# Modulation vectors of the second block: narrow products on TensorE, or dot products on VectorE in other stages

## The chip, the cores and the metric

The kernel runs on one core of one Trainium2 chip. The metric is the time of one execution on the device in microseconds (us), the median of several runs. Engines carry the profile's names: PE is TensorE's matmul, PEld its weight load, DVE is VectorE, ACT is ScalarE, POOL is GpSimd, SP is SyncE, which here only issues DMAs. L83 is line 83 of the kernel; the change shifts line numbers by a few, so that the same statement has another number afterwards.

## The reference, cut to what matters

A first block (a state-space mixer "s5" and a gated recurrence of 8 heads "hgrn2", merged, then a gated feed-forward stage) turns x and 16 meta tokens into x1. The second block modulates x1 and a context by vectors that come from two condition vectors of 1024 numbers each: `c` for the tokens, `c_ctx` for the context.

```python
def _adaln(cond, w_mod, b_mod):
    m = jax.nn.silu(cond) @ w_mod + b_mod        # w_mod: 1024 x 3072
    return jnp.split(m, 3, axis=-1)              # shift, scale, gate
...
        if i % 2 == 0:                           # layer "ab"
            sh, sc, gt = _adaln(c, ab_w_mod[j], ab_b_mod[j])
            h = x * (1.0 + sc[:, None]) + sh[:, None]
            ...
                csh, csc, cgt = _adaln(c_ctx, ab_w_mod[j], ab_b_mod[j])
                hc = ctx * (1.0 + csc) + csh
        else:                                    # layer "cd"
            csh, csc, cgt = _adaln(c_ctx, cd_w_mod[j], cd_b_mod[j])
            hc = ctx * (1.0 + csc) + csh
            sh, sc, gt = _adaln(c, cd_w_mod[j], cd_b_mod[j])
```

So four vectors of 3072 numbers are wanted: `c` and `c_ctx` through the ab weights, `c` and `c_ctx` through the cd weights. Of the last the gate is never used. None depends on x: they can be computed at any time before their use.

## The kernel before, in words

Features lie on the 128 partitions, tokens on the columns. Every float32 product is made of three float32r products: weights and inputs are split into a rounded part and a rest. `split_w` loads a raw 128x1024 tile into the pool `wraw` (two buffers; the DMA is issued by SP at L74), ACT copies its rounded part (L75), and DVE subtracts that from the raw tile (L76). `panel` then multiplies one such tile with all tokens (`mm3`, L83): 72 matmuls for the three token chunks of the first block, 24 for the 256 tokens of the context.

The stages of the program, in order:

- `s5`: eight passes. Each projects an input (one panel of L83), stores it to DRAM and reads it back in another layout, and DVE builds a table `ctab` (five operations, the last at L368) that PE transposes (L438). A scan over chunks on DVE and eight output passes end the stage.
- `hgrn`, the heads: eight heads, each with two panels of its own, a DVE chain (two scans over 1040 columns, L598 and L599, reciprocals, some twenty products, states), and about a hundred small matmuls; at its end DVE scales the output `o`, and SP stores it to `YBd` (L729). The second scan of the next head writes the tile `B`, which is the buffer of `o`: it waits until that store has landed. Other panels (`z_panel`: queries, values and gates wanted later) fill PE's time in the heads and after them; their number is fixed, so a panel that is done in a head is not to be done later.
- `ctx_path`: the context through layer ab and half of cd. Its own panels are small, and `fill` puts a `z_panel` between them.
- `merge`, `ffn` (ten groups of `up` and `down`; `up` is two panels and a convolution of three DVE operations per panel, `down` adds products into the residual on DVE at L951), then the second block on the tokens.

Around the change: `mods` is a generator that `hgrn` advances six times per head. For each of 48 tiles (2 layers x 3 parts x 8 input blocks) it loads 128 inputs x 1024 features into the pool `wm` (two buffers, L1015) and multiplies them with both conditions: the conditions, padded to 32 columns, are the stationary operand, and the weights stream past in four matmuls of 256 columns (L1017; in the trace eight records per tile). After eight tiles DVE copies the sums out, PE transposes them (L1024), and DVE adds the bias and forms 1 + scale and gate / ALPHA (L1027, L1029).

Each engine runs its instructions in one fixed order, and so does each queue of DMA issues. That order comes from the scheduler of the tile framework: it places every instruction by the data and buffers that it needs and by the order of the code, so an edit in one place can move instructions of others.

Of the kernel before, what the change touches and what calls it, by code (L numbers as in the profile page):

```python
# [19 lines left out]
NJ = 1026  # L20
# [17 lines left out]
class Build:  # L38
# [20 lines left out]
    # ---- weights: raw -> exact split into two float32r parts  # L59
# [8 lines left out]
    # the sources side by side into the two parts of t  # L68
# [9 lines left out]
    # X: function (part, k, lo, hi) -> AP ; W: tile [128, 2, nk*128]  # L78
# [18 lines left out]
    # rsqrt(ps * scale + eps), one Newton step on top of the table's value  # L97
# [30 lines left out]
    # exp(x) in place on a small tile, x clamped to [-87, 88]  # L128
# [26 lines left out]
    # sin(th + shift) with the range brought to [-pi, pi]; shift 0 or pi/2  # L155
    def exact_sin(self, pool, out, th, shape, shift):
# [25 lines left out]
    # ================= block 1 =================  # L182
# [20 lines left out]
    def block1(self, upto):  # L203
# [32 lines left out]
        # panel 1 (queries), 2 (values) of a head; 0: gates  # L236
# [33 lines left out]
    # panels chunk by chunk, where the chunks of X come one after the other  # L270
# [7 lines left out]
    def s5_params(self, pool, w1):  # L278
# [37 lines left out]
        # powers a^0..a^8, ascending (pa) and descending (pd)  # L316
# [18 lines left out]
        # bb = coef * b  # L335
# [10 lines left out]
        # scan multipliers [Ar|Ar], [-Ai|Ai]  # L346
# [7 lines left out]
    def cmul_tab(self, pool, pw, r0, r1, co, i):  # L354
        """out[128, 2, 4, 8, 16] = pw (over t) * co (over h) for the four pairs of panel i"""
# [15 lines left out]
    def s5(self):  # L371
# [5 lines left out]
        with ExitStack() as es:  # L377
# [17 lines left out]
            # first panels token chunk by token chunk, under the norm of the next chunk  # L395
# [3 lines left out]
            for c, (lo, hi) in enumerate(CH1):  # L399
                pss = [self.ps_mm()[:, 0:hi - lo] for _ in ws]  # L400
                # as the inputs of the first chunk come
# [18 lines left out]
            proj(2)  # L420
            for i in range(8):
                if i < 5:
                    proj(i + 3)
# [7 lines left out]
                # maps  # L431
# [28 lines left out]
                # chunk inputs to the states  # L460
# [7 lines left out]
            # outputs' factors, real and imaginary states on top of each other  # L468
# [6 lines left out]
            # scan over the chunks  # L475
# [9 lines left out]
            # outputs  # L485
            for i in range(8):
# [7 lines left out]
                # re(a^t c) over -im(a^t c)  # L494
# [24 lines left out]
    # ---- hgrn2  # L519
    def hgrn(self):  # L520
        nc, tc, A = self.nc, self.tc, self.A
        v = nc.vector
        with ExitStack() as es:
# [37 lines left out]
            wm = es.enter_context(self.pool("wm", 2, side="right"))  # L561
            mods = self.mods(wm, hp)
            for hd in range(8):
                # projections
# [5 lines left out]
                next(mods, None)  # L570
# [4 lines left out]
                next(mods, None)  # L575
                next(mods, None)
# [7 lines left out]
                next(mods, None)  # L584
                next(mods, None)
                next(mods, None)
# [6 lines left out]
                # decays inside the chunks of 16  # L593
# [16 lines left out]
                # queries and keys against the middle of their chunk of 32; QI: block, key chunk, query  # L610
# [3 lines left out]
                # meta chunk  # L614
# [8 lines left out]
                # chunk totals  # L623
# [9 lines left out]
                # queries decayed from the start of their chunk of 32, then from the middles of earlier chunks  # L633
# [7 lines left out]
                # products over the chunks of 16 before and after in the block of 128  # L641
# [36 lines left out]
                # states before each block  # L678
# [12 lines left out]
                # outputs  # L691
# [19 lines left out]
                # norm over the head's features, gate  # L711
                # (four token ranges side by side in the columns of the array, brought back by selections)
# [20 lines left out]
            for m in mods:  # L733
                pass

    # exact split of an fp32 tile into the two parts of t[:, :, lo:hi]
# [13 lines left out]
    # a product whose result goes on to a norm: the first panels panel by panel, the last nres  # L750
    # panels token chunk by token chunk, so that the norm of a chunk runs under the next chunk.
    # sq: the norm needs the sum of squares (else the plain sum) over all panels' rows r(i, lo, hi);
    # done(c, lo, hi, ps) gets that sum in every partition
# [68 lines left out]
    def merge(self):  # L822
# [5 lines left out]
        with ExitStack() as es:  # L828
# [50 lines left out]
            # h1 = h + (2 m) @ w_out / 2, then its norm  # L879
# [3 lines left out]
            # in place of the product's input, which a finished chunk no longer needs  # L883
# [19 lines left out]
    def ffn(self):  # L903
# [5 lines left out]
        with ExitStack() as es:  # L909
# [58 lines left out]
            for gi, js in enumerate(groups):  # L968
                for j in js[0:2]:
                    up(j)  # L970
                if gi:
                    down(groups[gi - 1], False)
# [21 lines left out]
    def mods(self, pool, cp):  # L994
# [13 lines left out]
        for which in ("ab", "cd"):  # L1008
            m = self.mod[which] = self.const.tile([128, 24, 2], F32, name=f"mod_{which}")
            bm = self.load(self.const, f"{which}_b_mod")  # L1010
            for part in range(3):
                ps = self.ps_sm()[:, 0:256]
                for k in range(8):
# [4 lines left out]
                    if k < 7:  # L1018
                        yield
# [793 lines left out]
```

## Time and profile before

| | |
|---|---|
| time, median of 3 runs | 3249.68 us (3247.68 to 3250.23) |
| span of the profiled execution | 3242.6 us, that is 7.1 us less than the median |
| PE busy | 3165.4 us, 98% of the span |
| DVE, ACT, POOL busy | 1831.4, 1126.1, 92.9 us |
| heads (first to last store of `YBd`) | 477.1 to 783.6 us |

The span runs from the first to the last instruction; the 7.1 us around it are outside the trace. In rows of a stretch the columns are its bounds, its length, then for PE, PEld, DVE, ACT and POOL the busy time (with the number of instructions), then the granted TensorE clock (1.00 is full speed), the busy share of the DMA engines and GB/s. In a timeline a row is the start, the time from the first start to the last end, engine, line and what it writes and reads; rows of the same kind in succession are put together with their count, and brackets give idle time before it and what ended it.

### The profile page before, as it was taken

The page shows a single profiled execution, that of the slowest core. Times are in us where ns is not written, and L with a number is a line of the kernel's source. Part 1 is how long each engine was busy: PE and PEld are TensorE (multiplying, and loading weights), DVE is VectorE, ACT ScalarE, POOL GpSimd, SP SyncE. Part 2 cuts the span into 40 slices and gives each one's busy share as a digit, 9 for nine tenths or more (in the row PEclk, how much of TensorE's full clock was granted, in tenths as well). Part 3 has the DMA queues.
Part 4 walks back from the last instruction along what each step waited for, and adds up shares of the span by engine and source line. Part 5 has one row for each costly group of instructions (what it writes and reads, how often), then busy time and mean ns, then how long its engine had stood idle before and what let it go on. Part 6 is the DMA issues. An engine that isn't in the chain of part 4 may idle for free.

```text
span 3242.6 us, 47786 instructions
## 1 busy us (share of the span) xinstructions
PE 3165.4 (98%) x19986; PEld 2840.8 (88%) x19986; DVE 1831.4 (56%) x3508; ACT 1126.1 (35%) x1846; POOL 92.9 (3%) x99
## 2 busy tenths in 40 slices
PE   8999899999999999999999999999999999999998
PEld 6999887879999999999999999989997889555476
DVE  7549468775454334465554555455336464777744
ACT  5341733233344312232222222252224353544532
POOL 0000000000210000000000000000000000121100
PEclk9999999999999999999999999999999999999999
DMA  4342454343552234111111111111111223000211
GB/s 153 90 161 91 148 182 142 118 153 103 158 155 81 91 118 130 33 59 46 40 46 53 47 52 40 53 35 54 46 40 66 92 88 130 29 7 7 79 49 52
DMA packets 106384, 269.01 MB, mean 83 GB/s; under 512 B 14798, under 2 KB 43694, under 8 KB 105974
## 3 DMA queue, kind: packets, MB, share of 16 engines
q1 hardware_dynamic: 99656, 245.35, 23.3%
q10 hardware_dynamic: 4464, 16.34, 1.3%
q0 software_dynamic: 2048, 4.26, 0.7%
q8 instruction: 157, 2.57, 0.3%
q14 instruction: 59, 0.48, 0.0%
HBM read 219.12 MB, written 46.11 MB: 82 GB/s over the span
## 4 chain that ended last, share of the span: by engine, by line
PE 90%; DVE 4%; DMA 2%; ACT 2%; issue 1%; SPq 0%; DVEq 0%; ACTq 0%
PE mm L83 62%; PE mm L949 7%; PE sm L1558 4%; PE mm L1555 4%; PE sm L813 2%; PE mm L1124 2%; PE sm L1531 1%; DMA YBd<-o 1%; PE mm L1516 1%; ACT Tt L502 1%; DVE R L604 1%; PE sm L465 1%; PE sm L1573 0%; PE sm L708 0%; PE sm L1017 0%
## 5 line engine op out<-in xcount | busy, mean ns | idle before, releaser
L83 PE MATMUL mm<-z,whl 128*128 128x256 f32 (+3 forms) x4032 | 682.9, 325 | 1.5 <-ACT z L231 1.0
L83 PE MATMUL mm<-a,whl 128*128 128x384 f32 (+1 forms) x4320 | 682.7, 319 | 1.6 <-ACT u L917 1.6
L83 PEld LDWEIGHTS mm<-a,whl 128*128 128x128 f32 x4320 | 678.5, 188 | 3.7 <-ACT u L917 1.9
L83 PEld LDWEIGHTS mm<-z,whl 128*128 128x128 f32 x4032 | 637.6, 189 | 36.8 <-issue 29.2
L76 DVE TENSOR_TENSOR whl<-wraw,whl 128x1024 fp32r<-128x1024 f32 (+2 forms) x258 | 302.6, 1178 | 221.1 <-ACT whl L75 220.3
L75 ACT CAST whl<-wraw 128x1024 fp32r<-128x1024 f32 (+2 forms) x258 | 260.6, 1014 | 341.8 <-PE mm L949 137.0
L83 PE MATMUL mm<-hx,whl 128*128 128x384 f32 (+1 forms) x2232 | 366.3, 322 | 7.7 <-ACT fx L1378 7.1
L83 PEld LDWEIGHTS mm<-hx,whl 128*128 128x128 f32 x2232 | 352.0, 189 | 16.8 <-ACT fx L1378 7.3
L949 PE MATMUL mm<-g,whl 128*128 128x384 f32 (+1 forms) x1584 | 257.9, 322 | 2.3 <-DVE f L951 1.2
L949 PEld LDWEIGHTS mm<-g,whl 128*128 128x128 f32 x1584 | 248.0, 188 | 13.9 <-issue 8.1
L83 PE MATMUL mm<-b,whl 128*128 128x384 f32 (+1 forms) x1152 | 180.9, 319 | 0.0
L83 PEld LDWEIGHTS mm<-b,whl 128*128 128x128 f32 x1152 | 180.8, 189 | 0.0
L917 ACT COPY u<-mm 128x384 f32<-128x384 f32 x132 | 58.3, 445 | 317.8 <-PE mm L83 317.8
L951 DVE TENSOR_TENSOR f<-f,mm 128x384 f32<-128x384 f32 (+1 forms) x240 | 118.3, 508 | 71.3 <-PE mm L949 70.4
L1556 ACT ACTIVATE P<-mm 128x512 f32<-128x512 f32 x160 | 94.7, 597 | 134.4 <-PE mm L1555 127.9
L83 PEld LDWEIGHTS mm<-y,whl 128*128 128x128 f32 x816 | 120.2, 188 | 13.1 <-issue 9.8
L83 PE MATMUL mm<-y,whl 128*128 128x256 f32 (+1 forms) x816 | 128.1, 312 | 1.4 <-ACT y L741 1.1
L1558 PE MATMUL sm<-P,m 128*64 128x512 f32 x320 | 128.0, 611 | 0.6 <-ACT P L1556 0.5
L1532 DVE TENSOR_REDUCE mx<-sm 128x1 f32<-128x512 f32 (+1 forms) x192 | 105.7, 595 | 39.7 <-PE sm L1531 38.4
L1555 PE MATMUL mm<-m,KB 97*128 97x512 f32 x420 | 121.7, 405 | 0.0
L1555 PEld LDWEIGHTS mm<-m,KB 97*128 97x128 f32 x420 | 75.6, 188 | 47.4 <-issue 33.3
L923 DVE TENSOR_SCALAR av<-u,conv_w,conv_b 128x1024 f32<-128x1024 f32 x22 | 17.9, 812 | 138.7 <-ACT u L917 138.7
(519 smaller groups left out, 3664.0 us busy)
## 6 DMA issues: line engine op xcount, KB each, us to landing
wraw<-w_up SPq DMA_DIRECT2D x44, 512.0 KB, 3.2
wraw<-w_h SPq DMA_DIRECT2D x32, 512.0 KB, 3.4
wraw<-ab_w SPq DMA_DIRECT2D x32, 512.0 KB, 3.4
wm<-ab_w_mod SPq DMA_DIRECT2D x24, 512.0 KB
wm<-cd_w_mod SPq DMA_DIRECT2D x24, 512.0 KB, 4.0
wraw<-w_down SPq DMA_DIRECT2D x22, 512.0 KB, 3.2
ut<-Ud SPq DMA_DIRECT2D x16, 520.0 KB, 4.5
gt<-Gd SPq DMA_DIRECT2D x16, 513.0 KB, 3.2
```

The source lines that it names most:

```text
L75: self.nc.scalar.copy(t[:, 0], raw)
L76: self.nc.vector.tensor_tensor(out=t[:, 1], in0=raw, in1=t[:, 0].bitcast(F32), op=ALU.subtract)
L83: nc.tensor.matmul(ps, W[:, wp, wofs + 128 * k:wofs + 128 * k + 128], X(xp, kofs + k, lo, hi), start=first and k == 0 and i == 0, stop=las ...
L813: nc.tensor.matmul(p4[32 * j:32 * j + 32], self.ones[:, 0:32], x, start=i < 4, stop=i - len(pend) + j + 5 >= m)
L917: return u, (self.split_w(A["w_up"][p], [1024]), lambda c, lo, hi, ps: nc.scalar.copy(u[:, lo:hi], ps))
L949: nc.tensor.matmul(ps, ws[j][:, wp, 128 * o:128 * o + 128], G[j][:, xp, lo:hi], start=n_ == 0 and i == 0, stop=n_ == len(js) - 1 and i == 2)
L951: v.tensor_tensor(out=h1[o][:, 2 + lo:2 + hi], in0=h1[o][:, 2 + lo:2 + hi], in1=ps, op=ALU.add)
L1124: nc.tensor.matmul(ps, X(xp, k, 128 * t, 128 * t + 128), wv[k // 4][:, wp, 256 * (k % 4):256 * (k % 4) + 256], start=k == 0 and i == 0, st ...
L1532: v.tensor_reduce(out=mx[:, qt, j:j + 1], in_=ps, axis=mybir.AxisListType.X, op=ALU.max)
L1555: nc.tensor.matmul(ps, K[0:97, kp, 128 * t:128 * t + 128], Q[0:97, qp, 512 * c:512 * c + 512], start=i == 0, stop=i == 2)
L1556: nc.scalar.activation(Pt[:, c], ps, AF.Exp, scale=scale)
L1558: nc.tensor.matmul(po[64 * c:64 * c + 64, :], vv(t)[:, 64 * h:64 * h + 64], Pt[:, c], start=t == 0, stop=t == KT - 1)
```

## The change

The vectors are formed on DVE: the weights now come transposed, 128 features on the partitions and the 1024 inputs on the columns, and one `tensor_tensor_reduce` multiplies such a tile with the condition (the same row in all partitions), sums over the columns, adds the bias, and writes one column of the result. A tile serves one condition only. It appears in the program as two DVE instructions, one of 128x1024 and one of 128x1. `mods` is advanced in three stages: in `s5` three tiles per pass (ab for `c_ctx`, 24 tiles, in the buffers `km`), in `ctx_path` three per `fill` (cd for `c_ctx` without the gate, 16 tiles, in the `wraw` buffers of the z panels), in `ffn` three per `up` (all six parts for `c`, 48 tiles, in `wraw`). That makes 88 tiles of 512 KB in place of 48. Each stage prepares its condition row with `cond_rows`. The rest of the difference is comments that went.

```diff
@@ s5 @@
             proj(2)
+            self.mod_start()
+            cr = self.cond_rows(w1.tile([128, 1024], F32, tag="ys", name="cr1", bufs=1), w1.tile([128, 1024], F32, tag="k2", name="crt", bufs=1), 1)
+            mods = self.mods([("ab", 0), ("ab", 1), ("ab", 2)], 1, cr, lambda: w1.tile([128, 1024], F32, tag="km", name=self.nm("wm")))
             for i in range(8):
+                for _ in range(3):
+                    next(mods)
@@ hgrn @@
-            wm = es.enter_context(self.pool("wm", 2, side="right"))
-            mods = self.mods(wm, hp)
...
-                next(mods, None)
-                next(mods, None)
...
-            for m in mods:
-                pass
@@ ffn @@
+            cr = self.cond_rows(wx.tile([128, 1024], F32, tag="whl", name="cr3"), tp.tile([128, 1024], F32, tag="acc", name="crt", bufs=3), 0)
+            mods = self.mods([(w, p) for w in ("ab", "cd") for p in range(3)], 0, cr,
+                             lambda: self.wraw.tile([128, NJ], F32, tag="wraw", name=self.nm("wm"))[:, 0:1024])
...
                     up(j)
+                    for _ in range(3):
+                        next(mods, None)
@@ mods @@
-                    nc.sync.dma_start(w, A[f"{which}_w_mod"][8 * part + k])
-                    for j in range(4):
-                        nc.tensor.matmul(ps[32 * j:32 * j + 32], cs[:, k], w[:, 256 * j:256 * j + 256], start=k == 0, stop=k == 7)
...
+    def cond_rows(self, t, tmp, col):
+        nc.sync.dma_start(t, self.A["cond"][col].partition_broadcast(128))
+        nc.scalar.activation(tmp, t, AF.Tanh, scale=0.5)
+        v.scalar_tensor_tensor(out=t, in0=tmp, scalar=1.0, in1=t, op0=ALU.add, op1=ALU.mult)
+        v.tensor_scalar(out=t, in0=t, scalar1=0.5, scalar2=None, op0=ALU.mult)
+        return t
+    def mods(self, todo, col, c, new):
+        for which, part in todo:
+            m = self.mod[which]
+            for f in range(8 * part, 8 * part + 8):
+                w = new()
+                nc.sync.dma_start(w, A[f"{which}_w_mod"][f])
+                v.tensor_tensor_reduce(out=w, in0=w, in1=c, scale=1.0, scalar=self.modb[which][:, f:f + 1],
+                                       op0=ALU.mult, op1=ALU.add, accum_out=m[:, f, col:col + 1])
+                if f % 8 == 7 and part:
+                    o = m[:, 8 * part:8 * part + 8, col]
+                    v.tensor_scalar(out=o, in0=o, scalar1=(1.0, 1.0 / ALPHA)[part - 1], scalar2=None, op0=(ALU.add, ALU.mult)[part - 1])
+                yield
@@ ctx_path @@
+            cr = self.cond_rows(cp.tile([128, 1024], F32, name="cr2", tag="csq"), wg.tile([128, NJ], F32, tag="wraw", name="crt")[:, 0:1024], 1)
+            mods = self.mods([("cd", 0), ("cd", 1)], 1, cr, lambda: wg.tile([128, NJ], F32, tag="wraw", name=self.nm("wm"))[:, 0:1024])
+            fill0 = fill
+            def fill():
+                fill0()
+                for _ in range(3):
+                    next(mods, None)
             self.ab_mixer(tp, yp, X, T, CH, half_out, fill)
+            list(mods)
+            fill = fill0
@@ inputs @@
-        D[f"{w}_w_mod"] = np.ascontiguousarray(f(f"{w}_w_mod_2")[0].reshape(8, 128, 3, 1024).transpose(2, 0, 1, 3)).reshape(24, 128, 1024)
+        D[f"{w}_w_mod"] = np.ascontiguousarray(f(f"{w}_w_mod_2")[0].T).reshape(24, 128, 1024)
```

Where it moves instructions. PE at the end of the last head: `ry` is the last head's 1 / deviation, `z_83` to `z_90` the eight tiles of the normed input, each `whl` the weights of a panel. Before:

```order
L727 MATMUL sm_7606<-ry_7594,idr 128x258
L727 MATMUL sm_7610<-ry_7594,idr 128x258 x2
L83 MATMUL mm_7817<-z_85,whl_7785 128x384
L83 MATMUL mm_7817<-z_86,whl_7785 128x384 x3
L83 MATMUL mm_7817<-z_87,whl_7785 128x384 x3
L83 MATMUL mm_7817<-z_88,whl_7785 128x384 x3
```

Now:

```order
L724 MATMUL sm_7340<-ry_7328,idr 128x258
L724 MATMUL sm_7344<-ry_7328,idr 128x258 x2
L83 MATMUL mm_7662<-z_87,whl_7604 128x386
L83 MATMUL mm_7662<-z_88,whl_7604 128x386 x3
L83 MATMUL mm_7662<-z_89,whl_7604 128x386 x3
L83 MATMUL mm_7662<-z_90,whl_7604 128x386 x3
```

Between these last matmuls of the heads and the first panel on the context (`hc`) stand 184 panel matmuls before, and 82 now (the ten shown in part and one panel of 72); the other 102 stand inside the heads now.

DVE in `s5`, at the first table `ctab` (`ctmp` is its scratch tile; `wm`, `cr_818` and `mod_ab` are a weight tile, the condition row and the result). Before:

```order
L365 TENSOR_TENSOR ctab_991<-ctab_991,ctmp_992 128x512
L363 TENSOR_TENSOR ctab_1153<-pd,bb 128x512
L367 TENSOR_TENSOR ctmp_992<-pd,bb 128x512
L366 TENSOR_TENSOR ctab_1153<-pd,bb 128x512
L368 TENSOR_TENSOR ctab_991<-ctab_991,ctmp_992 128x512
```

Now:

```order
L365 TENSOR_TENSOR ctab_1012<-ctab_1012,ctmp_1013 128x512
L366 TENSOR_TENSOR ctab_1012<-pd,bb 128x512
L367 TENSOR_TENSOR ctmp_1013<-pd,bb 128x512
L1022 ISA wm_1083,mod_ab<-wm_1083,cr_818,ab_b_mod_813 128x1024
L1022 ISA mod_ab 128x1
L368 TENSOR_TENSOR ctab_1012<-ctab_1012,ctmp_1013 128x512
```

The two operations on the second table went behind L368, and the fifth weight tile came ahead of it; four more such pairs and the two operations on the condition row stand further up.

DVE in `ffn`, in a down phase (`f` are tiles of the residual, `mm` sums of PE in PSUM). Before:

```order
L951 TENSOR_TENSOR f_12709<-f_12709,mm_15871 128x384
L951 TENSOR_TENSOR f_12803<-f_12803,mm_15879 128x384
L951 TENSOR_TENSOR f_12803<-f_12803,mm_15887 128x256
L76 TENSOR_TENSOR whl_16002<-wraw_16003,whl_16002 128x1024
L951 TENSOR_TENSOR f_12803<-f_12803,mm_15895 128x384
```

Now:

```order
L946 TENSOR_TENSOR f_12791<-f_12791,mm_14648 128x384
L1022 ISA wm_14901,mod_ab<-wm_14901,cr_13169,ab_b_mod_813 128x1024
L1022 ISA mod_ab 128x1
L946 TENSOR_TENSOR f_12791<-f_12791,mm_14656 128x256
L946 TENSOR_TENSOR f_12791<-f_12791,mm_14664 128x384
```

Of the six weight tiles of a group two stand between the 24 evictions of its down phase, the other four in the up phases.

## Rows read from the trace of the kernel before

**Rows 1.** The page: busy time by engine; the chain that ended last.

```profile
PE 3165.4 (98%) x19986; PEld 2840.8 (88%) x19986; DVE 1831.4 (56%) x3508; ACT 1126.1 (35%) x1846; POOL 92.9 (3%) x99
...
PE 90%; DVE 4%; DMA 2%; ACT 2%; issue 1%; SPq 0%; DVEq 0%; ACTq 0%
```

**Rows 2.** Groups by line, 423 to 783 us: busy us, mean ns, idle before.

```profile
L1017 PE MATMUL sm<-wm,conds 128*32 128x256 f32 x384 | 36.5, 389 | 7.1 <-DMA wm<-ab_w_mod 5.0 <-DMA wm<-cd_w_mod 2.1
```

**Rows 3.** Line L1017: what ended PE's idle time (us, times).

```profile
  DMA wm<-ab_w_mod: 10.4, 9
  DMA wm<-cd_w_mod: 6.8, 13
```

**Rows 4.** Timeline of PE, 440 to 455 us: start, duration, line, count.

```profile
441.97 0.64 PE L1017 MATMUL sm<-wm,conds 128*32 128x256 f32 x8
442.54 1.31 PE L83 MATMUL mm<-z,whl 128*128 128x384 f32 x6
```

**Rows 5.** Stretches from one store to the next: length, engines' busy, clock, DMA.

```profile
477.10:522.90 45.80, 42.26 (x368) 34.85 (x360) 33.87 (x68) 14.87 (x21) 0.00 (x0) 1.00 0.50 150
...
567.10:613.70 46.60, 42.45 (x336) 39.01 (x335) 34.61 (x69) 15.52 (x23) 0.00 (x0) 0.93 0.24 69
...
746.70:783.60 36.90, 35.88 (x297) 33.50 (x296) 22.62 (x40) 12.36 (x19) 0.00 (x0) 1.00 0.25 87
```

**Rows 6.** Waits of DVE, 423 to 783 us: total, times, longest.

```profile
DVE B L599 <- DMA YBd<-o: 34.3, 7, 6.2
DVE SC L704 <- PE sm L703: 11.4, 8, 2.9
```

**Rows 7.** Timeline of SP's issues, 743 to 753 us.

```profile
746.65 0.33 SPq L729 DMA_DIRECT2D YBd<-o  x1
748.27 0.33 SPq L74 DMA_DIRECT2D wraw<-w_g  x1
```

**Rows 8.** Timeline of DVE, 743 to 753 us.

```profile
746.49 0.17 DVE L1027 TENSOR_TENSOR mod_cd<-sm,cd_b_mod 128x16 f32<-128x16 f32 x1
...
751.16 2.33 DVE L599 TENSOR_TENSOR_SCAN B<-fm,dr 128x1040 f32<-128x1040 f32 x1 [2.95 <-DMA YBd<-o]
```

**Rows 9.** Timeline of PE, 564 to 586 us.

```profile
583.87 1.94 PE L671 MATMUL sm<-ident,B 128*128 128x128 f32 x8 [3.95 <-DVE B L660]
```

**Rows 10.** Timeline of PE, 780 to 815 us.

```profile
782.39 29.92 PE L83 MATMUL mm<-z,whl 128*128 128x384 f32 x184
```

**Rows 11.** Groups of DVE by form, 423 to 783 us.

```profile
L604 DVE RECIPROCAL R<-B 128x512 f32<-128x512 f32 x8 | 26.8, 3352 | 0.2
...
L598 DVE TENSOR_TENSOR_SCAN F<-fm,fr 128x1040 f32<-128x1040 f32 x8 | 18.5, 2317 | 0.0
```

**Rows 12.** Groups of DVE by form, 1400 to 2090 us.

```profile
L924 DVE SCALAR_TENSOR_TENSOR ag<-u,conv_w,ag 128x1024 f32<-128x1024 f32 x22 | 28.3, 1284 | 0.8
```

**Rows 13.** The page, costliest groups: a TENSOR_SCALAR of 1024 columns.

```profile
L923 DVE TENSOR_SCALAR av<-u,conv_w,conv_b 128x1024 f32<-128x1024 f32 x22 | 17.9, 812 | 138.7 <-ACT u L917 138.7
```

**Rows 14.** Timeline of DVE, 85 to 101 us.

```profile
94.07 0.68 DVE L366 TENSOR_TENSOR ctab<-pd,bb 128x512 f32<-128x512 f32 x1
94.67 0.68 DVE L368 TENSOR_TENSOR ctab<-ctab,ctmp 128x512 f32<-128x512 f32 x1
```

**Rows 15.** Timeline of PE, 95 to 101 us.

```profile
100.26 0.93 PE L438 MATMUL sm<-ident,ctab 128*128 128x128 f32 x7
```

**Rows 16.** Stretches of s5, of ctx_path and of one down phase.

```profile
100.00:200.00 100.00, 99.73 (x841) 92.81 (x841) 36.78 (x90) 38.89 (x71) 0.00 (x0) 1.00 0.39 103
900.00:1000.00 100.00, 98.86 (x722) 93.50 (x721) 57.45 (x116) 55.14 (x86) 8.38 (x16) 1.00 0.43 134
1746.20:1769.20 23.00, 23.00 (x147) 22.84 (x146) 17.39 (x29) 2.83 (x4) 0.00 (x0) 1.00 0.08 24
```

**Rows 17.** Timeline of PE, 812 to 850 us.

```profile
817.75 11.54 PE L83 MATMUL mm<-z,whl 128*128 128x256 f32 x72
...
835.09 11.54 PE L83 MATMUL mm<-z,whl 128*128 128x256 f32 x72
```

More of the change, by code (lines that the diff above doesn't have):

```diff
@@ L574, in hgrn @@
                 nc.scalar.activation(k, k, AF.Identity, scale=fbn[:, hd:hd + 1], bias=fb[:, hd:hd + 1])
-                next(mods, None)
-                next(mods, None)
                 for j, t in ((1, q), (2, vv)):
@@ L583, in hgrn @@
                         self.panel(w, self.zx, 8, CH1 if j == 2 else CHT, lambda c, lo, hi, ps: nc.scalar.copy(t[:, lo:hi], ps))
-                next(mods, None)
-                next(mods, None)
-                next(mods, None)
                 w = self.split_w(A["w_h"][4 * hd + 3], [1024])
@@ L991, in x1_chunk, with mod_start @@
             self.split_act(self.hx[k], lo, hi, t)
-    def mods(self, pool, cp):
+    def mod_start(self):
+        self.mod = {}
+        self.modb = {}
+        for which in ("ab", "cd"):
+            self.mod[which] = self.const.tile([128, 24, 2], F32, name=f"mod_{which}")
+            self.modb[which] = self.load(self.const, f"{which}_b_mod")
+    def cond_rows(self, t, tmp, col):
+        nc = self.nc
+        v = nc.vector
+        nc.sync.dma_start(t, self.A["cond"][col].partition_broadcast(128))
[3 more added lines that the diff above has]
+        return t
@@ L997, in mods @@
+    def mods(self, todo, col, c, new):
         nc, A = self.nc, self.A
         v = nc.vector
-        self.mod = {}
-        cd = self.load(self.const, "cond")
-        th = self.const.tile([128, 16], F32, name="condt")
-        nc.scalar.activation(th, cd, AF.Tanh, scale=0.5)
-        v.scalar_tensor_tensor(out=cd, in0=th, scalar=1.0, in1=cd, op0=ALU.add, op1=ALU.mult)
-        v.tensor_scalar(out=cd, in0=cd, scalar1=0.5, scalar2=None, op0=ALU.mult)
-        cs = cp.tile([128, 8, 32], F32, name="conds")
@@ L1006, in mods @@
-        v.memset(cs, 0.0)
-        v.tensor_copy(cs[:, :, 0:2], cd.rearrange("p (k c) -> p k c", c=2))
[L1008 to L1013, printed above, removed]
-                    w = pool.tile([128, 1024], F32, tag="wm", name=self.nm("wm"))
-                    nc.sync.dma_start(w, A[f"{which}_w_mod"][8 * part + k])
-                    for j in range(4):
-                        nc.tensor.matmul(ps[32 * j:32 * j + 32], cs[:, k], w[:, 256 * j:256 * j + 256], start=k == 0, stop=k == 7)
-                    if k < 7:
-                        yield
-                e = pool.tile([128, 1024], F32, tag="wm", name=self.nm("me"))[:, 0:256]
-                v.tensor_copy(e, ps)
-                pt = self.ps_sm()
-                for h in range(2):
-                    nc.tensor.transpose(pt[:, 128 * h:128 * h + 128], e[:, 128 * h:128 * h + 128], self.ident)
-                o = m[:, 8 * part:8 * part + 8].rearrange("p (j h) c -> p h j c", h=2)
-                b = bm[:, 8 * part:8 * part + 8].rearrange("p (j h) -> p h j", h=2).unsqueeze(3).to_broadcast([128, 2, 4, 2])
-                v.tensor_tensor(out=o, in0=pt[:, 0:256].rearrange("p (h j c) -> p h j c", h=2, j=4)[:, :, :, 0:2], in1=b, op=ALU.add)
-                if part:
-                    v.tensor_scalar(out=m[:, 8 * part:8 * part + 8], in0=m[:, 8 * part:8 * part + 8], scalar1=(1.0, 1.0 / ALPHA)[part - 1],
-                                    scalar2=None, op0=(ALU.add, ALU.mult)[part - 1])
@@ L1031, in mods @@
                 yield
-            self.dump("mod_" + which, m)
     def ln_chunk(self, tp, r, ps, n, emit, sqt, tail):
@@ L1223, in ctx_path @@
                 ps = add(k, x[:, k])
-            sqs = cp.tile([128, 4, T], F32, name="csq")
+            sqs = cp.tile([128, 4, T], F32, name="csq", tag="csq")
             self.ln_chunk(tp, lambda k: x[:, k], ps, T, emit, lambda k: sqs[:, k % 4], 0)
@@ L1740, in prep @@
     D["fin_g"] = pk(f("final_norm_g"))
-    D["cond"] = np.ascontiguousarray(np.stack([pk(f("c_2")[0]), pk(f("c_ctx_2"))], 2).reshape(128, 16))
+    D["cond"] = np.ascontiguousarray(np.stack([f("c_2")[0].reshape(1024), f("c_ctx_2").reshape(1024)], 0))
     for w in ("ab", "cd"):
-        D[f"{w}_w_mod"] = np.ascontiguousarray(f(f"{w}_w_mod_2")[0].reshape(8, 128, 3, 1024).transpose(2, 0, 1, 3)).reshape(24, 128, 1024)
+        D[f"{w}_w_mod"] = np.ascontiguousarray(f(f"{w}_w_mod_2")[0].T).reshape(24, 128, 1024)
         D[f"{w}_b_mod"] = pk(f(f"{w}_b_mod_2")[0])
```

## Prediction, made before the changed kernel had run

> **What bounds the kernel now.** I read the page first. PE is busy for 98% of the span, and the chain that ended last runs 90% through PE and 4% through DVE [rows 1]: whatever comes off PE's work or its idle time is a gain, and DVE, busy for 56%, costs something only where PE waits for it. Next came the groups of the heads, where the removed products stand: 384 matmul records of L1017, 36.5 us busy [rows 2]. Busy time of pipelined matmuls overlaps with the neighbours', so I take the price from the timeline: the eight records of a tile start at 441.97, and the next panel matmul starts at 442.54, 0.57 us later [rows 4]. 48 tiles are 27.4 us of PE. Before them PE also idled for 10.4 and 6.8 us, until their weights had landed [rows 3], 17.2 us. Together 44.6 us, which is the most that PE can get back from the removal.
>
> Then I asked whether PE is what a head waits for. From one store of `YBd` to the next a head takes 45.8 or 46.6 us, with PE busy 42.3 and 42.5 and DVE 33.9 and 34.6 [rows 5]; the mean of the six from 477.1 to 746.7 is 44.93. Neither engine is full. DVE's waits name the chain: it stood 34.3 us before its second scan, until the store of the head before had landed [rows 6], and 11.4 us for PE's scores (L704). The head is a chain store, scan, DVE, PE, DVE, store, with panels around it. [...]
>
> **What goes, in the heads.** (1) The store's wait. In six heads the weight loads stand in SP's queue beside the store, and the scan waited (34.3 - 2.95) / 6 = 5.2 us. Around the last store, at 746.65, SP issued no `wm` load, only a panel's weights [rows 7], and the scan waited 2.95 us [rows 8]. I take the last head's wait for all: 6 x 2.3 = 13.6 us (bounds: 0, as loads of panel weights remain in the queue, to 6 x 5.2 = 31). (2) DVE's waits for PE, where weight products stood ahead of a head's own ones: bounds 0 and 11.4; I take 0.6 us a head, 3.4 in six, near the lower end, since the head with hardly any of these products was no faster. (3) The end. Between the last head's matmuls and the context's first panel stand 184 panel matmuls before and 82 now, as the order shows. The 184 took 29.92 us [rows 10], so 102 of them are 16.6 us that are no longer to be done there; PE does them in the heads, 14 or so a head. That PE has the time: 42.4 - 27.4 / 8 + 14 x 0.163 = 41.3 us of work against 44.9 - 2.8 = 42.1 per head. What now hides the context's first DVE operations behind the last head is 82 matmuls, 13.3 us, in place of 184; by bounds that costs 0 to 5, I take 0. The heads give 13.6 + 3.4 + 16.6 = 33.6, below the ceiling of 44.6.
>
> **What comes: one tile on DVE.** No row shows a multiply that sums over its columns. From below: a TENSOR_SCALAR of 1024 columns takes 0.81 us [rows 13]; from above: the RECIPROCAL, 3.35 us for 512 columns, so 6.7 for 1024 [rows 11]. Between them a SCALAR_TENSOR_TENSOR of 1024 columns with two float32 sources takes 1.28 [rows 12] and a scan over 1040, which carries a sum along, 2.32 [rows 11]. The nearest in operands and length is the 1.28; with 0.17 for the second instruction, of one column, as for an operation of 16 columns [rows 8], I take p = 1.45 us per tile, 88 tiles, 128 us of DVE work in all.
>
> [...]
>
> **s5.** DVE finishes the first table at 94.67 + 0.68 = 95.35 [rows 14] and PE, which has panels to do, takes it up at 100.26 [rows 15]: 4.9 us in hand. Ahead of it now stand the condition's two operations (1.28 + 0.81) and five tiles, while two operations of the second table (0.6 apart) went behind: 2.1 + 5p - 1.2 - 4.9 = 5p - 4.0, 3.3 us at p = 1.45; I take 4, as two buffers hold five tiles and the third to fifth wait for a load (bounds 0 and 10). The other passes: DVE is busy 36.8 of 100 us and PE 99.7 [rows 16]; a pass is a panel of 72 and some 60 smaller matmul records, and 841 took 100 us, so it takes 15.7, of which DVE has 9.9 free and gets 3p = 4.4. Cost 0 up to p = 3.3. Behind a weight load that waits for its buffer SP queues the input panel's weights and the eight stores of the pass; PE is behind them only when that wait is longer than a panel.
>
> **ctx_path.** A panel in front of 48 context matmuls, 817.75 to 835.09, is 17.3 us [rows 17], and DVE is busy 57.5 of 100 [rows 16], 10 of these 17.3; three tiles are 4.4 more, 14.4 of 17.3. It fits up to p = 2.5, but evictions stand in the queue behind the tiles, and the z panels' weights share their two buffers with them; 0 to 8 us, I take 2.5.
>
> **ffn.** A down phase of 23.0 us has DVE busy for 17.4 [rows 16], 5.6 free, and two tiles, 2.9 us, now stand between its 24 evictions; the other four stand where DVE waits for a panel. PE has four PSUM buffers, so that one delayed eviction doesn't stop it. Fits up to p = 2.8; 0 to 5 us, I take 0.5.
>
> **The sum.** -33.6 + 4 + 2.5 + 0.5 = -26.6 us, against the profiled execution: 3242.6 - 26.6 = 3216.0 of span; with the 7.1 us that the median has beyond this span 3223.1, so 3223 us. If each term is off by the bounds that I find plausible, this case runs from 3213 to 3233.
>
> **Rivals.** A, the head's chain is DVE's own and loads of panels keep the store as late as before: periods stay 44.9, only the end's 16.6 us remain, less 7 is -9.6: 3240. For it: the head at 567.1, long without weight tiles; against it: its clock was low, and the last store's wait was short. If PE idles more in the heads and all six get the clock of that one, 1.7 us each (46.6 - 44.9), it ends at 3250, no change.
>
> B, the new instruction is long, and DVE becomes the bound. Place: s5, the context and the down phases. Price: 5p - 4 at the first table, 16 tiles of ctx_path beyond 2.5, 16 tiles in down phases beyond 2.8, 19 in s5 beyond 3.3, and 2.5. It equals 33.6 at p = 3.2, from which point the kernel is slower; at p = 4 it is 16 + 24 + 19 + 13 + 2.5 = 75, and 3250 - 34 + 75 = 3291 us. For it only that the operation is unknown, and the RECIPROCAL's 3.35 for half the columns; against it the two-source row at 1.28.
>
> C, PE gets everything back, 44.6, and the additions hide but for 3 us at the first table: 3208. For it PE's 98%; against it DVE's 34 us of work and the store's latency in each head.
>
> D, SP's queue: a weight load that waits for DVE holds back the loads and stores behind it, and PE waits for the panel's weights at each of the 24 tiles of s5 as it did for a weight tile in the heads, 10.4 / 9 = 1.2 us [rows 3]: 28 us, the gain is gone: 3251. Against it: PE's 99.7% there says that its weights come early [rows 16].
>
> **How the numbers follow.** Chances: forecast 0.50, C 0.14, A 0.20, B 0.08, D 0.08. This kernel's measurement can tell 0.2%, 6.5 us, from no change. Faster takes all of the forecast and of C, 0.12 of A and 0.02 of D: 0.78. Same takes 0.05 of A and 0.03 of D: 0.08. Slower is B with 0.03 each of A and D: 0.14. The range for 8 in 10 goes from C's far side, 3204, to the top of A without a low clock, 3246.
>
> **What would show it.** In the trace after: no L1017; stores of `YBd` about 42 us apart and the scan's wait near 3 us (in A 45 and 5); a panel stretch of some 13 us behind the last head in place of 29.9; L1022 at about 1.3 us (in B over 3); PE idle before L438's counterpart, about 4 us; DVE at 83% in ctx_path with PE still at 98%; down phases still 23 us. The prediction is wrong if the tile takes over 2.5 us, or if a head's period is above 44.

## The result: 1% slower, where 0.8% faster was forecast

The changed kernel takes 3280.48 us (median; 3278.04 to 3285.44), the kernel before, run beside it, 3248.68. The ratio is 1.0108 (95% interval 1.0093 to 1.0122), outside the range and on the other side. The profiled execution has a span of 3283.6 us, 41.0 more than before. It is the longest of its four executions, and the one before, to judge by its span, the shortest of its four (3244.17 us), so the stretches below add up to 9 us more than the 31.8 between the medians.

The page of the kernel after, busy time by engine and the chain that ended last, answering to [rows 1]:

```profile
PE 3148.6 (96%) x19590; PEld 2848.1 (87%) x19590; DVE 1938.4 (59%) x3677; ACT 1131.5 (34%) x1849; POOL 93.6 (3%) x99
...
PE 83%; DVE 8%; DMA 5%; ACT 3%; issue 2%; SPq 0%; DVEq 0%; ACTq 0%
```

PE's busy time fell by 17 us, and it is busy for 96% of the span in place of 98%; 8% of the chain runs through DVE and 5% through DMAs, where they had 4 and 2. Work went and waits came. To see where, I take the first or last start of one line in each stage (views of one line) and subtract before from after:

| stretch | before | after | change | forecast |
|---|---|---|---|---|
| start to the first output product of s5 | 362.9 | 406.4 | +43.5 | +4 |
| from there over the heads to the context's first panel | 449.2 | 413.0 | -36.2 | -33.6 |
| ctx_path, first to last panel on the context | 178.0 | 196.9 | +18.9 | +2.5 |
| ffn, first copy of `u` to first eviction of a down phase | 75.4 | 93.0 | +17.6 | +0.5 with the next |
| all the rest | 2177.1 | 2174.3 | -2.8 | 0 |

**The heads did what was forecast.** From 518.4 to 769.4 a head takes 41.8 us on average (42.1 was forecast). First one such stretch, answering to [rows 5], then the waits of DVE for the store, answering to [rows 6], then the panels behind the last head, answering to [rows 10]:

```profile
518.40:559.20 40.80, 37.97 (x312) 35.38 (x311) 34.59 (x67) 15.45 (x23) 0.00 (x0) 1.00 0.23 66
```

```profile
DVE B L596 <- DMA YBd<-o: 23.2, 7, 5.0
```

```profile
806.23 13.28 PE L83 MATMUL mm<-z,whl 128*128 128x386 f32 x82
```

The scan waited 23.2 us for the stores in place of 34.3, and 82 panel matmuls take 13.28 us in place of 184 in 29.92.

**The new instruction costs what was forecast.** The view of its line; duration min/median/max, then what its engine waited for:

```profile
L1022 DVE CUSTOM_DVE_ANT_0 wm<-wm,cr,ab_b_mod x48: 1270/1284/1286, 84.9 to 1628.9; 128x1024 f32<-128x1024 f32 x48
L1022 DVE DVE_READ_ACCUMULATOR2_ANT mod_ab<- x48: 75/84/86, 86.1 to 1630.1; 128x1 f32 x48
...
  DMA wm<-cd_w_mod: 64.3, 29
  DMA wm<-ab_w_mod: 33.9, 21
```

1.28 + 0.08 = 1.37 us a tile; p was 1.45. With two float32 sources and an accumulator it takes as long as the two-source row without one, 1284 ns in both [rows 12]. But DVE, in order, stood 98.2 us in front of it until its tile had landed, and that had no term in my sum.

**s5: the panel's weights come late.** PE's timeline, answering to [rows 15], shows the first table costing 0.76 us (3.3 to 4 were forecast), and then something else:

```profile
100.78 0.98 PE L443 MATMUL sm<-ident,ctab 128*128 128x128 f32 x7 [0.76 <-DVE ctab L368]
...
160.73 2.10 PE L83 MATMUL mm<-z,whl 128*128 128x256 f32 x6 [4.89 <-ACT whl L75]
...
186.08 2.08 PE L83 MATMUL mm<-z,whl 128*128 128x256 f32 x6 [5.97 <-ACT whl L75]
...
209.98 2.08 PE L83 MATMUL mm<-z,whl 128*128 128x256 f32 x6 [5.63 <-ACT whl L75]
...
233.52 2.08 PE L83 MATMUL mm<-z,whl 128*128 128x256 f32 x6 [5.27 <-ACT whl L75]
...
255.71 150.89 PE L83 MATMUL mm<-z,whl 128*128 128x256 f32 x936 [5.11 <-ACT whl L75]
```

Five times PE waits 4.9 to 6.0 us, 26.9 in all, for ACT to have split a panel's weights. Backwards from the first of these, on ACT, SP and DVE:

```profile
159.64 1.05 ACT L75 CAST whl<-wraw 128x1024 fp32r<-128x1024 f32 x1 [4.89 <-DMA wraw<-w_in]
```

```profile
152.92 0.33 SPq L464 DMA_DIRECT2D KKd<-kk  x1
154.21 0.33 SPq L1021 DMA_DIRECT2D wm<-ab_w_mod  x1
154.59 0.43 SPq L74 DMA_DIRECT2D wraw<-w_in  x1
```

```profile
151.87 0.27 DVE L447 MEMSET cb<- 128x256 f32 x1 [8.43 <-PE sm L455]
...
152.90 1.27 DVE L1022 CUSTOM_DVE_ANT_0 wm<-wm,cr,ab_b_mod 128x1024 f32<-128x1024 f32 x1
```

The weights (`w_in`) were issued at 154.59, behind a tile (L1021, 154.21) whose buffer DVE gave back with the product that began at 152.90, which stands behind a MEMSET that had waited 8.43 us for PE, and behind the store of `kk` (152.92), which waits for PE too. So PE waits for weights whose load waits for PE. In SP's order each panel's weights now stand a pass further back, and from the panel that PE first waited for on, two. Before:

```
L430 DMA ut_1151<-Ud 128x1040
L459 DMA KKd<-kk_1032 128x128
L74 DMA wraw_1385<-w_in 128x1024
L430 DMA ut_1313<-Ud 128x1040
L459 DMA KKd<-kk_1194 128x128
```

After:

```
L464 DMA KKd<-kk_1224 128x128
L1021 DMA wm_1422<-ab_w_mod 128x1024
L1021 DMA wm_1425<-ab_w_mod 128x1024
L435 DMA ut_1352<-Ud 128x1040
L1021 DMA wm_1428<-ab_w_mod 128x1024
L74 DMA wraw_1433<-w_in 128x1024
```

`wraw_1385` and `wraw_1433` are the weights of the same panel: they stood between the first and the second store of `kk`, and now they stand behind the second (the eight stores of `u` are left out). The next weights, those of the panel at 160.73, were issued behind the second store of `kk` before, and now stand behind the fourth (the rows at 152.92 and 154.59 above). Before:

```profile
119.59 0.34 SPq L459 DMA_DIRECT2D KKd<-kk  x1
...
122.42 0.38 SPq L74 DMA_DIRECT2D wraw<-w_in  x1
```

Their panel began at 151.94, 29.5 us after the issue; now it begins 6.1 us after it. The waits have a second price, the clock. The stretch between the first two:

```profile
160.70:186.00 25.30, 18.65 (x129) 16.54 (x129) 10.00 (x21) 6.48 (x12) 0.00 (x0) 0.84 0.43 128
```

It was granted 0.84 to 0.88 of full speed from 160.7 to 255.7, where s5 had 1.00 before [rows 16]: PE was idle 5 us, and in steps of 2 us the granted clock then reads 0.50 from 160 to 166, 0.93 in the next step, and 1.00 from 168 on until PE is idle again. The sum of s5: from the first table's transposes to the first output product PE has 1440 panel matmuls before and after. That took 262.6 us with 0.3 of waits before, and takes 306.7 with 32.0 now, 26.9 of them the five and 5.1 small ones. The remaining 12.4 us are slower matmuls; the table came 0.5 us sooner, which leaves 43.5. (95 us at a mean of 0.86 would make 13, an estimate that counts PE's idle time in and leaves out the 44 us behind, at 0.93.)

**ctx_path.** Here PE waited 13.4 us in all for the subtraction of panel weights (12.9 on L83, 0.5 on L1119), against 1.2 before. The total, and the second longest of these waits on PE, SP and DVE:

```profile
PE mm L83 <- DVE whl L76: 12.9, 5, 4.8
```

```profile
844.35 4.92 PE L83 MATMUL mm<-hc,whl 128*128 128x256 f32 x22 [4.45 <-DVE whl L76]
```

```profile
831.43 12.09 SPq L1021 DMA_DIRECT2D wm<-cd_w_mod  x3
844.33 0.33 SPq L74 DMA_DIRECT2D wraw<-ab_w  x1
```

```profile
841.87 1.28 DVE L1022 CUSTOM_DVE_ANT_0 wm<-wm,cr,cd_b_mod 128x1024 f32<-128x1024 f32 x1 [4.25 <-DMA wm<-cd_w_mod]
...
843.08 1.22 DVE L76 TENSOR_TENSOR whl<-wraw,whl 128x1024 fp32r<-128x1024 f32 x1
```

DVE stood 4.25 us in front of the tile, and the subtraction of weights that PE wanted (L76) stood behind it. SP could issue the three tiles only over 12.09 us, the last when the product of 841.87 was through; the weights of 844.33 behind them are for a later panel.

**ffn.** One wait, 14.36 us, in the first group; the down phases are untouched, 22.75 us, answering to [rows 16]:

```profile
1446.64 71.03 PE L83 MATMUL mm<-a,whl 128*128 128x384 f32 x432 [14.36 <-ACT whl L75]
1517.52 22.75 PE L944 MATMUL mm<-g,whl 128*128 128x384 f32 x144
```

```profile
1426.39 0.33 SPq L1005 DMA_DIRECT2D cr<-cond  x1
1439.10 0.33 SPq L1021 DMA_DIRECT2D wm<-ab_w_mod  x1
1441.51 2.91 SPq L74 DMA_DIRECT2D wraw<-w_up  x2
```

The second up's weights were issued at 1441.51, behind a tile whose buffer came free with a product that needed the condition row, which was loaded only at 1426.39. The kernel before issued them at 1407.94:

```profile
1407.94 3.38 SPq L74 DMA_DIRECT2D wraw<-w_up  x2
```

The other 3 us are the clock: it was 0.76 in the 13.4 us behind the wait, and 1.00 in this stretch before.

### The profile page after: what moved, and what is told of

The parts are those of the page before. It is cut to its first block, busy times and chain, and to the rows that moved or that the text cites. A ratio compares the mean times of both kernels' runs of the same rounds, so it can differ in the third digit from the quotient of the medians.

```text
span 3283.6 us, 47234 instructions
## 1 busy us (share of the span) xinstructions
PE 3148.6 (96%) x19590; PEld 2848.1 (87%) x19590; DVE 1938.4 (59%) x3677; ACT 1131.5 (34%) x1849; POOL 93.6 (3%) x99
## 4 chain that ended last, share of the span: by engine, by line
PE 83%; DVE 8%; DMA 5%; ACT 3%; issue 2%; SPq 0%; DVEq 0%; ACTq 0%
PE mm L83 56%; PE mm L944 7%; PE sm L1563 4%; PE mm L1560 4%; PE sm L808 2%; PE mm L1119 2%; DMA wm<-cd_w_mod 2%; PE sm L1536 1%; DMA YBd<-o 1%; DVE R L601 1%; PE mm L1521 1%; ACT Tt L507 1%; DVE whl L76 1%; DMA wraw<-w_h 1%; DVE wm L1022 1%
## 5 line engine op out<-in xcount | busy, mean ns | idle before, releaser
L83 PE MATMUL mm<-z,whl 128*128 128x256 f32 (+3 forms) x4032 | 684.2, 328 | 31.5 <-ACT whl L75 26.9
L83 PE MATMUL mm<-a,whl 128*128 128x384 f32 (+1 forms) x4320 | 686.0, 320 | 14.9 <-ACT whl L75 14.4
L83 PEld LDWEIGHTS mm<-a,whl 128*128 128x128 f32 x4320 | 681.2, 189 | 17.6 <-ACT whl L75 14.6
L83 PEld LDWEIGHTS mm<-z,whl 128*128 128x128 f32 x4032 | 648.6, 193 | 52.5 <-ACT whl L75 28.5
L76 DVE TENSOR_TENSOR whl<-wraw,whl 128x1024 fp32r<-128x1024 f32 (+2 forms) x258 | 303.2, 1178 | 212.8 <-ACT whl L75 212.2
L83 PE MATMUL mm<-hx,whl 128*128 128x384 f32 (+1 forms) x2232 | 366.6, 322 | 7.7 <-ACT fx L1383 7.1
L83 PEld LDWEIGHTS mm<-hx,whl 128*128 128x128 f32 x2232 | 352.4, 190 | 16.8 <-ACT fx L1383 7.3
L944 PEld LDWEIGHTS mm<-g,whl 128*128 128x128 f32 x1584 | 245.2, 188 | 14.7 <-issue 8.1
L83 PE MATMUL mm<-b,whl 128*128 128x384 f32 (+1 forms) x1152 | 180.9, 319 | 0.0
L83 PEld LDWEIGHTS mm<-b,whl 128*128 128x128 f32 x1152 | 180.8, 189 | 0.0
L83 PEld LDWEIGHTS mm<-y,whl 128*128 128x128 f32 x816 | 121.0, 191 | 18.9 <-issue 9.8
L83 PE MATMUL mm<-y,whl 128*128 128x256 f32 (+1 forms) x816 | 129.0, 314 | 6.9 <-DVE whl L76 4.8
L1537 DVE TENSOR_REDUCE mx<-sm 128x1 f32<-128x512 f32 (+1 forms) x192 | 105.7, 596 | 39.7 <-PE sm L1536 38.4
L1022 DVE CUSTOM_DVE_ANT_0 wm<-wm,cr,cd_b_mod 128x1024 f32<-128x1024 f32 x40 | 51.4, 1284 | 64.6 <-DMA wm<-cd_w_mod 64.3
```

The lines of the kernel that those rows point to most:

```text
L76: self.nc.vector.tensor_tensor(out=t[:, 1], in0=raw, in1=t[:, 0].bitcast(F32), op=ALU.subtract)
L83: nc.tensor.matmul(ps, W[:, wp, wofs + 128 * k:wofs + 128 * k + 128], X(xp, kofs + k, lo, hi), start=first and k == 0 and i == 0, stop=las ...
L944: nc.tensor.matmul(ps, ws[j][:, wp, 128 * o:128 * o + 128], G[j][:, xp, lo:hi], start=n_ == 0 and i == 0, stop=n_ == len(js) - 1 and i == 2)
L1022: v.tensor_tensor_reduce(out=w, in0=w, in1=c, scale=1.0, scalar=self.modb[which][:, f:f + 1], op0=ALU.mult, op1=ALU.add, accum_out=m[:, f, ...
L1537: v.tensor_reduce(out=mx[:, qt, j:j + 1], in_=ps, axis=mybir.AxisListType.X, op=ALU.max)
```

## The experiments

Theories: Q, a queue or engine in order holds panel weights behind a tile; W, DVE's 88 products are in the way; T, the traffic of 40 more tiles. All runs were timed in three rounds beside the kernel before. The table at the end has all of them by stretch.

**Through another queue.**

```diff
-                nc.sync.dma_start(w, A[f"{which}_w_mod"][f])
+                nc.gpsimd.dma_start(w, A[f"{which}_w_mod"][f])
```

> The changed kernel with the 88 weight tiles of the vectors loaded through GpSimd's DMA queue; nothing else is edited, buffers and DVE's products stay. Theory Q (the queue): the panels' own weights come late because SP's queue is in order and holds them behind a weight tile whose buffer DVE has not released. Then in s5 the five waits of 5 to 6 us of PE before a panel and the low clock after them go, 40 of the 43 us that s5 lost; in ctx_path and at the start of ffn the tiles still share two buffers with panel weights, so that half of the 19 and most of the 17.6 us stay: about 3240 us. Theory W (work: 88 x 1.37 us on DVE are in the way): no change, 3280. Theory T (traffic: 40 more tiles of 512 KB): no change, 3280.

3243.8 us, 1.0003 (0.9993 to 1.0012) of before. s5 loses 8.0 in place of 43.5; ctx_path keeps 14.3 and ffn 17.7. With the same products on DVE and the same bytes, W and T fall for s5. Why ctx_path keeps its loss, though the queue is free, the longest wait of PE there shows, on PE, ACT, SP and DVE:

```profile
833.58 2.08 PE L83 MATMUL mm<-z,whl 128*128 128x256 f32 x6 [7.91 <-ACT whl L75]
```

```profile
832.48 2.19 ACT L75 CAST whl<-wraw 128x1024 fp32r<-128x1024 f32 x3 [4.86 <-DMA wraw<-w_g]
```

```profile
824.86 0.33 SPq L74 DMA_DIRECT2D wraw<-w_g  x1
```

```profile
823.54 1.28 DVE L1022 CUSTOM_DVE_ANT_0 wm<-wm,cr,cd_b_mod 128x1024 f32<-128x1024 f32 x1
```

Here it is the shared buffer: SP issued the panel's weights (`w_g`) only when a tile's product, ended at 824.82, had given the buffer back, they landed 7.6 us later, and PE waited 7.91.

**Products without loads.**

```diff
-                nc.sync.dma_start(w, A[f"{which}_w_mod"][f])
-                v.tensor_tensor_reduce(out=w, in0=w, in1=c, scale=1.0, ...
+                v.tensor_tensor_reduce(out=w, in0=c, in1=c, scale=0.001, ...
```

> The changed kernel without the 88 loads; the product on DVE takes the condition row twice and writes into the same buffers, so its values are not the reference's. DVE's work and the claim on the buffers stay, SP's queue is free. Theory Q: s5 back at the time of before, ctx_path loses under 8 of its 19 us, and the first group of ffn keeps some 12 of its 17.6, since the panel weights there wait for the buffers: about 3230 us. Theory W: 3280. Theory T: about 3215, all losses gone.

3231.36 us, 0.996 (0.9945 to 0.9974). s5 +6.8, ctx_path +0.1, ffn's first group +16.3. So ctx_path's loss needs the tiles' loads: without them, products and their claim on buffers cost nothing there; and ffn's is not the loads. What is left in s5 is mostly DVE's work: PE waits 4.4 us for the first table, about the 4 that were forecast.

**Loads with a product of one column.**

```diff
-                v.tensor_tensor_reduce(out=w, in0=w, in1=c, scale=1.0, ... accum_out=m[:, f, col:col + 1])
+                v.tensor_tensor(out=m[:, f, col:col + 1], in0=w[:, 0:1], in1=c[:, 0:1], op=ALU.mult)
```

> The changed kernel with all 88 loads on SP, but DVE multiplies only one column of each tile (0.1 us in place of 1.37), so the vectors are not the reference's. Theory Q: the loads still wait for a buffer that an instruction in DVE's order releases, and most of the loss stays, 3260 to 3280 us. Theory W: the losses go, 3215. Theory T: 3275 or more.

3272.99 us, 1.0094 (1.007 to 1.0118). s5 +35.8, ctx_path +14.7, ffn +14.0: with hardly any work on DVE most of the loss stays. W is out as the main price, and by the run through the other queue so is T in s5. For ctx_path the runs do not part T from waits for single tiles; that it is the waits rests on the traces.

**Nothing in place of the products** (loads, products and condition rows deleted, the vectors set by a MEMSET).

> The changed kernel without loads, products and condition rows; the vectors are set to a constant, so the output is not the reference's. What the removal from the heads alone gives. The heads of the changed kernel were 37 us shorter than before, so all theories expect 3249 - 37 = 3212 us (3205 to 3218); a time near 3230 would say that part of those 37 us was only moved from another stage.

3203.65 us, 0.9873 (0.9859 to 0.9888): 40 us in place of the 37 expected, under the ceiling of 44.6 that the prediction had.

**Panel first in s5.**

```diff
-                for _ in range(3):
-                    next(mods)
                 if i < 5:
                     proj(i + 3)
                 for _ in range(FS5.get(i, 0)):
                     self.z_panel(w1, "u", 4)
+                for _ in range(3):
+                    next(mods)
```

> The changed kernel with one edit in s5: the three tiles of a pass stand behind that pass's panel in the program, not ahead of it; all loads stay on SP. Theory Q (SP's queue is in order, and the panel's weights stand behind a tile that waits for DVE): the order alone cures it, s5 up to its output products takes 363 + 8 to 12 us in place of 406, and ctx_path and ffn lose as before: 3280 - 33 = 3247 us. Rival U (it is the stores and loads of u behind the tiles, or DVE's products themselves, that hold the pass): they stay behind the tiles, s5 stays above 395, 3270 to 3280.

3270.38 us, 1.0071 (1.0051 to 1.009); s5 393.4. The time is U's, and s5 lies 1.6 under U's bound, far from Q's 371 to 375: the order of the code is not enough. In SP's order only the first of the later panels came back ahead of its store of `kk`; the next ones still stand a pass late or more, behind tiles of the pass before.

**The store of `kk` through GpSimd**, and the same with the panel first:

```diff
-                nc.sync.dma_start(KKd[i, 0:128, :], kk)
+                nc.gpsimd.dma_start(KKd[i, 0:128, :], kk)
```

> The changed kernel with the small store of kk (L464) issued by GpSimd in place of SP. In SP's order of the changed kernel the weights of a panel stand one pass further back than before, behind that store, which waits for PE and DVE, and behind a tile (L1021), which waits for DVE. If the store is what holds them, s5 up to its output products falls from 406 to 375 us or less and the time to 3250; if the tile holds them by itself (theory Q), s5 stays above 395 and the time above 3268.

> The kernel with the panel first in s5 (it had 393 us there) and the store of kk issued by GpSimd besides: no tile of its own pass and no store of kk ahead of a panel's weights. If these two are all that holds the weights, s5 comes to 375 or less, 3250 us; if tiles of the pass before and the read of u behind them hold on, above 385, 3262 to 3270.

3271.0 us (1.0079, 1.0063 to 1.0094) with s5 at 392.5, and 3264.59 (1.0057, 1.0042 to 1.0072) with s5 at 385.9, the first between the two theories in s5 and the second just inside what was said for tiles of the pass before. So moving the store was worth 14 us of the 43.5, moving the tiles behind the panel 13, both together 20.5, and all but 8.0 goes when the tiles leave the queue. What holds the 23 us that are left with both moved was not tried by itself. Its trace shows more than the queue: PE waited longer for the subtraction of weights on DVE than for their cast.

```profile
PE mm L83 <- DVE whl L76: 7.9, 4, 4.1
PE mm L83 <- ACT whl L75: 5.2, 5, 2.0
```

In front of the longest of these, 4.1 us, ACT had long cast the weights, and L76 stood on DVE behind table operations that had waited 6.48 us for PE.

**Late start in ffn.**

```diff
-            cr = self.cond_rows(wx.tile(...), ...)
-            mods = self.mods(...)
...
                     up(j)
-                    for _ in range(3):
+                    for _ in range(3 if gi else 0):
                         next(mods, None)
+                if gi == 0:
+                    cr = self.cond_rows(wx.tile(...), ...)
+                    mods = self.mods(...)
```

> The changed kernel with one edit in ffn: condition row and tiles start after the first group's two up stages, so that no tile is ahead of the second up's weights (the 48 tiles go into groups 1 to 8). Theory Q: PE's wait of 14.4 us in the first group goes, since up's third and fourth panel weights no longer stand behind tiles that wait for the condition row; first group 75 to 77 us in place of 93.0, the later groups as before: 3280 - 17 = 3263 us. Rival B (the tiles' claim on the two shared buffers costs in every group, the first only shows it): the wait moves to the second group, 3280.

3267.95 us, 1.0065 (1.005 to 1.008). The first group takes 75.4 us again, and the other groups with all 48 tiles are as before: the loss was the wait for the condition row at the start, and the tiles cost nothing where the row is there.

**All cures.** Tiles through GpSimd, behind the panel in s5, five a pass there, none in ctx_path, late start in ffn:

> All cures together: tiles through GpSimd's queue, behind the panel in s5, five per pass there (the 40 tiles for the context, none in ctx_path), and the late start in ffn. Theory Q: heads and the panels behind them keep their gain of 36 to 40 us; s5 loses 8 to 14, as in the run through GpSimd's queue (8) with 16 tiles more; ctx_path and ffn lose nothing: 0.3 to 0.9% under before, about 3216 us on the chip where before took 3244. Theory W (DVE's products are the price): s5 with 40 tiles loses more than 30, no gain left.

> The same as the run before it, but the tiles go through SP's queue again, behind the panel's weights. If only the place in the order counts, within 5 us of it, about 3219; if a second queue is worth more (stores of u and loads back behind the tiles), s5 loses 20 or more and it comes to 3230 to 3240.

3228.32 us, 0.9941 (0.9923 to 0.996), faster than both kernels. ctx_path and ffn lose nothing, but s5 loses 23.1, more than the 8 to 14 expected, and the time is 12 us above the 3216. On SP's queue the same kernel takes 3260.49, 1.0045 (1.0031 to 1.006), with s5 at +55.5, 20 us above both numbers expected: here the queue alone is worth 32 us.

**Three buffers in s5** (the third in place of `k2`, idle there):

> The run with all cures (3228 against 3245 of before, s5 386) with three buffers in place of two for the tiles in s5. Its DVE waits 1 to 2 us for most tiles, since a load of 4.7 us and a product of 1.4 with two buffers allow one tile in 3 us and a pass of 16 us wants five. If that is the price, s5 falls to 375 or less and the time by 10 us, to 3216; if it is DVE's products (5 x 1.4 us a pass), s5 stays at 383 or more.

3227.58 us, 0.9937 (0.9921 to 0.9954). s5 falls from 386.0 to 376.9, between the two; in this profile the heads lose more than that (-27.8 in place of -40.1; why stays open), and the times do not differ. So 9 of those 23 us was the waiting for tiles; what is left includes the first table, for which PE now waits:

```profile
108.30 0.69 PE L443 MATMUL sm<-ident,ctab 128*128 128x128 f32 x2 [5.85 <-DVE ctab L365]
```

All runs, change of each stretch against before in the profiled execution (us):

| run | s5 | heads | ctx_path | ffn, first group | rest | time / before |
|---|---|---|---|---|---|---|
| changed kernel | +43.5 | -36.2 | +18.9 | +17.6 | -2.8 | 1.0108 |
| other queue | +8.0 | -38.4 | +14.3 | +17.7 | -2.9 | 1.0003 |
| no loads | +6.8 | -37.5 | +0.1 | +16.3 | -4.1 | 0.996 |
| one column | +35.8 | -34.3 | +14.7 | +14.0 | -3.8 | 1.0094 |
| nothing | -0.6 | -37.0 | -0.1 | 0.0 | -3.2 | 0.9873 |
| panel first | +30.5 | -38.3 | +18.3 | +16.4 | -1.6 | 1.0071 |
| late in ffn | +44.6 | -35.5 | +19.3 | 0.0 | -3.7 | 1.0065 |
| all cures | +23.1 | -40.1 | -1.0 | 0.0 | -3.6 | 0.9941 |
| all, on SP | +55.5 | -38.2 | 0.0 | -0.1 | -2.5 | 1.0045 |
| `kk` by GpSimd | +29.6 | -34.8 | +19.4 | +16.9 | -1.5 | 1.0079 |
| first, and `kk` | +23.0 | -37.1 | +18.1 | +17.1 | -1.9 | 1.0057 |
| three buffers | +14.0 | -27.8 | +0.7 | -0.1 | -2.3 | 0.9937 |

## Why the prediction was wrong

- **The gain was right.** The heads gave 36.2 us where 33.6 were summed, and the terms are near their measures: the period 41.8 against 42.1, the stores' waits 11.1 less against 13.6, DVE's waits for scores 4.5 less against 3.4 (the head with hardly any weight products, on which that forecast leaned, is the one from 567.1 in [rows 5]), the 102 matmuls 16.6 as forecast. The ceiling of 44.6 was misread: [rows 3] add the idle time of PE, 7.1 [rows 2], and that of PEld, 10.1, which overlaps PE (busy for 88% and 98% of the span [rows 1]). PE's own sum is 27.4 + 7.1 = 34.5; the 36.2 lie above it, so other waits shrank too.
- **The price of a tile was right**, 1.37 us against 1.45, and so was the bound that the down phases have room for two.
- **The step that failed is the one that priced DVE's work and the place on DVE, and not the queue.** It said of s5: "Behind a weight load that waits for its buffer SP queues the input panel's weights and the eight stores of the pass; PE is behind them only when that wait is longer than a panel." The condition was wrong. The waits of SP at the tiles are short (11.8 us in seven in s5, where it stood some 80 us in front of stores of `kk`), but the order had put a panel's weights one or two passes further back, so that the panel's time of lead was gone before any wait began, and the instruction that frees the tile's buffer stands behind waits for PE. Measured +43.5 against +4. I had the changed order of SP to read, and did not count where the weights of a given panel stand against the stores of `kk`.
- **Rival D named this mechanism** and gave it 28 us, at 0.08. The idle time that it priced was 26.9 us, but that the numbers meet is luck: D counted 24 waits of 1.2 us, and there were five of 5.4. What it did not have is the clock, 12 us more, and the same mechanism in two other stages. Its counter-argument, PE's 99.7% there, spoke of the kernel before, whose order it was not about.
- **ctx_path, 2.5 forecast and 18.9 measured.** I asked whether DVE has time for three tiles (it has: without loads the stage loses 0.1), and not what stands in DVE's order behind a product whose tile is still on its way. The two shared buffers were named, with 0 to 8 us.
- **ffn, 0.5 forecast and 17.6 measured.** The steady groups cost nothing, as said. The first group was not worked out at all: there the products need a row that is loaded and formed only when the stage begins.
- **The 7.1 us outside the trace were misread.** In the twelve other runs on record the profiled execution took 1.7 to 2.5 us more than its span; the rest of the 7.1 is that the median was of other, longer executions. From 3244.17, the execution of four that fits the span, the forecast would have been 3218, as far off.

## What to carry to other kernels

A load or product that is added to a stage with idle time is priced by its place in the queues that it shares, before its own duration (here the same 24 tiles cost s5 43.5 us on SP's queue and 8.0 on another): find in the new order, for each transfer that the bounding engine needs, which waiting instruction now stands ahead of it, and count in passes, not in microseconds. Loads that nobody waits for go to a queue whose other entries nobody waits for either. A stage's first pass wants its own line in the sum (ffn lost 17.6 us in its first group, and none of it with the late start).

## What the runs showed of the hardware

- In 95 us of s5 with five waits of PE of 4.9 to 6.0 us the granted clock was 0.84 to 0.88, where it was 1.00 before; the slower matmuls, 12.4 us, cost about half as much again as the waits. In the run through the other queue, without these waits, it was 1.00 there.
- From the issue of a head's store to the scan that waited for it went 6.2 to 8.2 us in the six heads with weight tiles in the queue, 4.5 in the one without, and 4.8 to 5.5 in the changed kernel. The scans behind the stores of 477.1 before and 518.4 after:

```profile
485.24 2.33 DVE L599 TENSOR_TENSOR_SCAN B<-fm,dr 128x1040 f32<-128x1040 f32 x1 [6.20 <-DMA YBd<-o]
```

```profile
523.37 2.33 DVE L596 TENSOR_TENSOR_SCAN B<-fm,dr 128x1040 f32<-128x1040 f32 x1 [2.95 <-DMA YBd<-o]
```

- The same 88 loads, issued by GpSimd in place of SP, brought the time from 1.0108 to 1.0003 of before, some 34 us, and the loss of s5 from 43.5 us to 8.0.
